# Low parts in quarter tiles, stacked products of the last 16 keys, softmax sums spread by transfers, and an end without GpSimd, in a two-layer attention and retention trunk

## The chip, the cores and the metric

The kernel runs on one core of a Trainium2 chip. The metric is the device time of one execution in microseconds; a figure for a kernel is the median of its runs. Five engines work side by side and meet through semaphores: PE (TensorE, matrix products and transposes), DVE (VectorE), ACT (ScalarE), POOL (GpSimd) and SP (SyncE, which here only issues transfers).

## The reference, cut to what matters

Sixteen learned meta tokens are put ahead of 512 tokens, so every layer has 528 positions of width 1024. Two layers run one after the other:

```python
proj = rmsnorm(h) @ w_in                     # 1024 -> 3*512 + 8 + 4*512 columns
fq, fk, fv, flog, rq, rk, rv, rg = split(proj)
# forgetting attention: 8 heads of 64, c = cumsum(log_sigmoid(flog + b))
s = fq.fk / 8 + c[t] - c[s], causal;  fox = softmax(s) @ fv
# retention: 4 heads of 128, gamma_h ** (t - s), chunked; rq, rk rotated
ret = silu(rg) * groupnorm((rq.rk * decay) @ rv)
h = h + concat(fox, ret) @ w_out
h = h + (silu(rmsnorm(h) @ w_gate) * (rmsnorm(h) @ w_up)) @ w_down
# behind both layers: out = rmsnorm(h)[:, 16:]
```

All of it is float32. The kernel reaches that accuracy with products of split operands: a number is written as a high part, rounded to the short form that TensorE takes at full rate, and a low part, the rest. A product is then high by high, high by low, and low by high, added up in PSUM.

## The kernel before, in words

Tokens lie along the free dimension: `h[k]` holds 128 features by 528 tokens. A dense projection (`dense_steps`, L190) is one job for each 128 output columns: its weights come by a transfer on SP as `raw` (128 partitions by 8 blocks of 128 columns, three buffers), `convert` (L160) casts half of it, 128x512, at a time to the high part `whi` on ACT (L186), and subtracts that from `raw` to get the low part `wlo` (L187). 63 of the 84 dense jobs have `pool` set and do that subtraction on GpSimd, the others on DVE. Then each of eight blocks runs three products, `xh`·`whi`, `xl`·`whi` and `xh`·`wlo`, in two column halves of 264 (L210).

Forgetting attention goes by pairs of heads, g = 0 to 3 (`fox_steps`, L460). For both heads s of a pair, and for query blocks of 128 (in layer 0 with a block of the 16 meta queries ahead), `scores` makes the logits on PE, takes the row minimum of their negative on DVE, and the exponential with its row sum on ACT (L517). `turn` transposes the probabilities on PE and splits them into `pth` and `ptl` (DVE L138). `product` multiplies them with the values `vv`, whose high and low columns lie side by side in one 128-column weight, so that a key block j takes two matmuls (L567; the 16 meta queries have their own, L559). Keys come in four blocks of 128 and one of the last 16 (`KOFF`, `KLEN`). Behind the second head the result is multiplied by the reciprocals of the row sums: they are taken on DVE (L525), spread to 64 columns a head by an ACT copy (L527), turned by four PE transposes (L576), and multiplied from PSUM (L577).

Retention has four heads `hd` (`ret_steps`, L648): scores times the decay (L699), a split into `rsh` and `rsl` (L138), and three products for each key block (L724), for the last 16 keys too, out of tiles of their own (`end_tiles`). Its queries and keys are rotated before that (L608 to L613: two ACT copies, two DVE products and a DVE addition, L613).

The order of PE's instructions is written out by hand: the attention steps of one pair are spread between the dense chunks of the next (`merge`, `spread`), so that PE has dense work while ACT and DVE work on the scores. The order on the other engines comes from a list scheduler with priorities and some pinned instructions. The FFN of each layer (L863 to L1017) uses no GpSimd.

At the end of the last layer (`after_a` to `after_7`, L1135 to L1213) the final norm is laid between the last products of the FFN, in two parts of the tokens: a (272 columns) and b (240). The sums of squares are gathered on DVE (`sum_b`), summed over partitions on PE (`sums`, L1135), and the inverse root is an `Ln` and an `Exp` on ACT (`root`) with a Newton step on DVE (`newton`, L1127 to L1131). The multiplications `out_a` and `out_b` (L1110) go to GpSimd for features 0 to 3 of part a and 6 to 7 of part b, to DVE for the others; SP sends each pair out (L1113).

Of the kernel before, what the change touches and what calls it, by code (L numbers as in the profile page):

```python
# [10 lines left out]
F32 = mybir.dt.float32  # L11
# [28 lines left out]
def hybrid_kernel(ctx, tc, x_t, w_in, w_fl, w_out, w_gate, w_up, w_down, vecs, b_fg, rope, decay, mask, ident, out_t):  # L40
# [25 lines left out]

    p_tiles, t_tiles, pm_tiles, v_tiles, end_tiles, low_keys = [], [], [], [], [], []
# [13 lines left out]
    def enter_att(l):  # L81
# [11 lines left out]
        for t in t_tiles:  # L93
            nc.gpsimd.memset(corners(t).bitcast(F32), 0.0)
        pm_tiles[:] = [phase["att"].tile([32, 32], F32, name=f"pm{i}") for i in range(2)] if l == 0 else []
        for t in pm_tiles:
            zero(l, t)
        end_tiles[:] = [[phase["att"].tile([128, META], F32R, name=f"rs{i}{k}") for k in range(2)] for i in range(2)]
        for t in end_tiles[0] + end_tiles[1]:
            zero(l, t.bitcast(F32))  # L100
# [4 lines left out]
    def corners(t):  # L105
        return t.rearrange("p j c -> p (j c)").rearrange("p (n c) -> p n c", c=META)[:, ::(T + 128) // META]

# [52 lines left out]
    def convert(j, upto=NK, pinned=False):  # L160
# [18 lines left out]
        while job["split"] < min(n, upto):  # L179
# [7 lines left out]
            pin(sub(lo, job["raw"][:, c0:c1], hi.bitcast(F32)), pinned)  # L187
# [209 lines left out]
    def silu(t, last=False):  # L397
        nc.scalar.activation(t, t, AF.Silu)
        if last:
            tc.keep_in_program_order(nc.scalar.preload_act_table_set("natural_log_exp_and_others"))  # L400
# [12 lines left out]
    def fox_dense(l, g, ly, real, st):  # L413
# [32 lines left out]
        def v_done(ps):  # L446
            vt = v_tiles[0]
            for t, (c0, c1) in zip(ps, FULL):
                nc.vector.scalar_tensor_tensor(vt[:, c0:c1], t[:, 0:c1 - c0], RSC, ly["R"][:, c0:c1],
                                               ALU.mult, ALU.mult)  # L450
            st["vt"] = vt
# [8 lines left out]
    def fox_steps(g, st, ly, real):  # L460
# [21 lines left out]
        def scores(s, b):  # L482
# [29 lines left out]
            else:  # L512
                if (s, b) == (0, 0):
                    st["sums"] = tmp.tile([128, NBLK, 2], F32, name="sums", tag="sums")
                rsum = st["sums"][:, b, s:s + 1]
# [8 lines left out]
            elif (s, b) == todo[-1]:  # L524
                nc.vector.reciprocal(st["sums"], st["sums"])  # L525
# [10 lines left out]
        def turn(s, b):  # L536
# [4 lines left out]
            if b < 0:  # L541
                e = at("pe", F32, (32, NBLK, 32), 2)[:, 0]
                nc.vector.transpose(e, info[s, b])
                split(pth[0:META, 0, 0:META], ptl[0:META, 0, 0:META], e[0:META, 0:META])
# [3 lines left out]
            if b == blocks[-1]:  # L548
                split(*[corners(t)[0:META, 1:] for t in (pth, ptl)], st["ends"][0:META, :, 32 - META:32])

        def product(s):
# [4 lines left out]
            if not real:  # L556
                po = psum_a()
                for i, pp in enumerate(pt):
                    nc.tensor.matmul(po[:, 0:META], v[:, 0, :], pp[:, 0, 0:META], start=(i == 0), stop=(i == 1))  # L559
# [4 lines left out]
            for j in range(5):  # L564
                c0 = max(0, KOFF[j] - META)
                for i, pp in enumerate(pt):
                    nc.tensor.matmul(po[:, c0:SEQ], v[:, j, :], pp[:, j, META + c0:T],  # L567
                                     start=(j == 0 and i == 0), stop=(j == 4 and i == 1))
# [3 lines left out]
            if s == 1:  # L572

                rb = psum_a()
                for b in range(NBLK):
                    nc.tensor.transpose(rb[:, 128 * b:128 * b + 128], st["rows"][:, 128 * b:128 * b + 128], idt)  # L576
                nc.vector.tensor_mul(mt[:, META:T], rb, mt[:, META:T])  # L577
# [24 lines left out]
    def ret_dense(l, hd, ly, real, st, which):  # L602
# [17 lines left out]
        def v_done(ps):  # L620
            vr = v_tiles[1]
            nc.vector.scalar_tensor_tensor(sv(vr, False), pv(ps, False), RSC, sv(ly["R"], False), ALU.mult, ALU.mult)
            st["vr"] = vr

        def g_done(ps):
# [3 lines left out]
            if hd > 1:  # L629
                silu(sv(sg, real), True)  # L630
# [17 lines left out]
    def ret_steps(l, hd, st, real):  # L648
# [5 lines left out]
        def values():  # L654
# [3 lines left out]
            for j0, n, p3 in transpose_into(st["vr"], KOFF):  # L658
# [5 lines left out]
                split(vh[:, j0:j0 + n], vl[:, j0:j0 + n], c)  # L664
# [6 lines left out]
        def scores(grp):  # L671
# [32 lines left out]
            if full < used:  # L704
                eh, el = end_tiles[hd % 2]
                split(eh[0:kn], el[0:kn], sd[0:kn, full:used])
                kept["e"] = (eh, el)
            kept["t", grp[0]] = (sh, sl)

        def product(grp):  # L710
# [5 lines left out]
            for j in grp:  # L716
# [4 lines left out]
                if j == 4:  # L721
                    (sh, sl), used = kept["e"], 0
                for i, (a, b) in enumerate(((vh, sh), (vh, sl), (vl, sh))):
                    nc.tensor.matmul(po[:, qa - META:SEQ], a[:, j, :], b[:, used + qa - q0:used + T - q0],  # L724
                                     start=(j == 0 and i == 0), stop=(j == 4 and i == 2))
# [62 lines left out]
    def ffn(l, st, real, last):  # L788
# [93 lines left out]
        class Unit:  # L882
# [64 lines left out]
            def done(self):  # L947
# [6 lines left out]
                silu(sg[:, c], self.f == NF - 1)  # L954
# [103 lines left out]
        else:  # L1058
# [49 lines left out]
            def out(eng, y, r, k, c0, c1):  # L1108
                pair = r.unsqueeze(1).broadcast_to([128, 2, c1 - c0])
                f = eng.tensor_mul(y, y, pair)  # L1110
                if eng is nc.vector:
                    pin(f)
                nc.sync.dma_start(out_t[k:k + 2, :, c0 - META:c1 - META].rearrange("k p c -> p k c"), y)  # L1113

            def out_a(eng, k):
                out(eng, fin["ya"][k // HB][:, k % HB:k % HB + 2], fin["ra"], k, *PA)

            def out_b(eng, k):
                out(eng, fin["yb"][:, k:k + 2], fin["rb"], k, *PB)

            def root(r, v):
                pin(nc.scalar.activation(r, v, AF.Ln, bias=epsc, scale=1.0 / D))
                pin(nc.scalar.activation(r, r, AF.Exp, scale=-0.5))
# [43 lines left out]
            def after_3():  # L1167
                a = fin["ra"], fin["va"], fin["ta"]
                sum_b(2)
                newton(0, *a)  # L1170
                newton(1, *a)
                square_b(3)
                scale_b(0, 1)

            def after_4():
                newton(2, fin["ra"], fin["va"], fin["ta"])
# [226 lines left out]
```

## Time and profile before

| | |
|---|---|
| median of 3 runs | 1278.69 us (1278.58 to 1278.84) |
| the profiled execution | 1278.89 us, its span 1277.1 us |
| mean granted TensorE clock | 0.996 |
| PE busy | 1258.0 us, 99% of the span, 9265 instructions |
| DVE, ACT, POOL busy | 1019.4, 687.7, 181.0 us |
| moved by DMA | 120.55 MB |

The span goes from the first to the last recorded instruction or transfer; the execution's own time is 1.79 us longer than its span. Start times in the views are microseconds from the start of the span. A matmul's recorded duration overlaps that of the next, so what one costs in a stream is read from the distance between the starts. Layer 0's attention lies at about 21 to 282 us, its output projection and FFN at 282 to 650, layer 1's attention at 650 to 905, its projection and FFN behind that, and the end of the last layer from 1248 on.

### The profile page before, as it was taken

Reading aid. Unit: us, or ns where it says so; the run is one execution under the profiler, and the core shown is the slowest. Engines: PE = TensorE matmul, PEld = TensorE weight load, DVE = VectorE, ACT = ScalarE, POOL = GpSimd, SP = SyncE. Lnnn points to the kernel's source line nnn. Section 1 sums busy time; section 2 is a strip of 40 time slices with the busy share of each in tenths; the row PEclk is TensorE's granted clock in tenths of the full one; section 3 lists DMA queues with packets and bytes.
Section 4 is the critical chain, followed back from the end, with each engine's and each line's share of the span. In section 5 each row is a group of like instructions: output and inputs, shape, how many; then the busy total and the mean of one; then the engine's idle time right before and its main releaser. Section 6 shows DMA issues by size and latency. Waiting matters only on the chain.

```text
span 1277.1 us, 23190 instructions
## 1 busy us (share of the span) xinstructions
PE 1258.0 (99%) x9265; PEld 1197.8 (94%) x9265; DVE 1019.4 (80%) x1849; ACT 687.7 (54%) x1250; POOL 181.0 (14%) x150
## 2 busy tenths in 40 slices
PE   9999999999999999999999999999999999999997
PEld 8899999999999999999999989999789999999996
DVE  7888866879988888887687878568899878888867
ACT  7566655576544444444455665456764444444445
POOL 2233333210000000000014334332000000000001
PEclk9999999999999999999999999999999999999998
DMA  6222222223323333332323122222223333333321
GB/s 233 76 67 84 75 84 84 66 73 115 107 97 100 100 100 100 100 100 83 100 76 112 65 100 84 77 91 66 100 83 130 102 100 100 100 100 100 103 79 67
DMA packets 45677, 120.55 MB, mean 94 GB/s; under 512 B 5360, under 2 KB 12272, under 8 KB 45568
## 3 DMA queue, kind: packets, MB, share of 16 engines
q1 hardware_dynamic: 45136, 118.77, 28.4%
q8 instruction: 73, 1.20, 0.4%
q10 hardware_dynamic: 432, 0.29, 0.1%
q14 instruction: 36, 0.29, 0.1%
HBM read 116.91 MB, written 2.13 MB: 93 GB/s over the span
## 4 chain that ended last, share of the span: by engine, by line
PE 84%; DVE 10%; ACT 4%; DMA 1%; issue 1%; DVEq 0%; POOL 0%; ACTq 0%
PE psd L210 24%; PE psa L875 18%; PE psd L1010 14%; PE psd L875 13%; PE psa L1010 4%; PE psa L210 3%; PE psa L409 2%; PE psa L497 1%; PE psa L567 1%; PE psa L724 1%; PE psa L694 1%; DVE qs L429 1%; DMA bc<-cdr 1%; DVE pr L504 1%; DVE rsl L138 0%
## 5 line engine op out<-in xcount | busy, mean ns | idle before, releaser
L187 POOL TENSOR_TENSOR wlo<-raw,whi 128x512 fp32r<-128x512 f32 x126 | 172.3, 1381 | 380.2 <-ACT whi L186 380.2
L210 PE MATMUL psd<-xh,whi 128*128 128x264 f32 (+1 forms) x792 | 195.8, 315 | 0.0
L210 PE MATMUL psd<-xl,whi 128*128 128x264 f32 (+1 forms) x792 | 186.5, 303 | 0.6 <-DVE xl L313 0.6
L210 PE MATMUL psd<-xh,wlo 128*128 128x264 f32 (+1 forms) x792 | 186.9, 303 | 0.0
L210 PEld LDWEIGHTS psd<-xh,whi 128*128 128x128 f32 x792 | 128.7, 190 | 4.7 <-ACT whi L186 0.4
L210 PEld LDWEIGHTS psd<-xh,wlo 128*128 128x128 f32 x792 | 127.2, 188 | 6.2 <-DVE wlo L187 0.4
L210 PEld LDWEIGHTS psd<-xl,whi 128*128 128x128 f32 x792 | 128.0, 189 | 5.2 <-DVE xl L313 1.2
L186 ACT CAST whi<-raw 128x512 fp32r<-128x512 f32 (+1 forms) x168 | 98.3, 613 | 39.2 <-PE psd L210 19.9
L863 ACT CAST whi<-raw 128x1024 fp32r<-128x1024 f32 (+2 forms) x62 | 54.9, 885 | 51.3 <-PE psd L875 39.9
L863 ACT CAST fwhi<-raw 128x1024 fp32r<-128x1024 f32 (+2 forms) x62 | 55.6, 897 | 48.1 <-PE psd L875 40.5
L864 DVE TENSOR_TENSOR wlo<-raw,whi 128x1024 fp32r<-128x1024 f32 (+2 forms) x62 | 62.9, 1014 | 13.7 <-ACT whi L863 13.6
L864 DVE TENSOR_TENSOR fwlo<-raw,fwhi 128x1024 fp32r<-128x1024 f32 (+2 forms) x62 | 64.0, 1032 | 10.8 <-ACT fwhi L863 10.5
L875 PE MATMUL psa<-th,whi 128*128 128x264 f32 (+1 forms) x232 | 65.4, 282 | 0.0
L875 PE MATMUL psa<-th,wlo 128*128 128x264 f32 (+1 forms) x232 | 65.4, 282 | 0.0
L875 PE MATMUL psa<-tl,whi 128*128 128x264 f32 (+1 forms) x232 | 65.3, 282 | 0.0
L875 PE MATMUL psa<-th,fwhi 128*128 128x264 f32 (+1 forms) x224 | 63.4, 283 | 0.0
L875 PE MATMUL psa<-tl,fwhi 128*128 128x264 f32 (+1 forms) x224 | 63.3, 283 | 0.0
L875 PE MATMUL psa<-th,fwlo 128*128 128x264 f32 (+1 forms) x224 | 63.3, 282 | 0.0
L517 ACT ACTIVATE pr<-pr,nmax 128x144 f32<-128x144 f32 (+1 forms) x64 | 36.9, 576 | 42.8 <-DVE nmax L504 30.5
L941 ACT COPY e<-psa 128x264 f32<-128x264 f32 (+1 forms) x114 | 42.9, 376 | 27.9 <-PE psa L875 23.6
L863 ACT CAST fwhi<-S 128x1024 fp32r<-128x1024 f32 x20 | 21.0, 1049 | 68.6 <-PE psa L875 66.5
L1010 PE MATMUL psd<-ah,fwlo 128*128 128x264 f32 (+1 forms) x200 | 56.6, 330 | 0.0
(355 smaller groups left out, 4008.6 us busy)
## 6 DMA issues: line engine op xcount, KB each, us to landing
raw<-w_in SPq DMA_DIRECT2D x54, 512.0 KB, 3.5
raw<-w_gate SPq DMA_DIRECT2D x44, 512.0 KB, 4.0
fraw<-w_up SPq DMA_DIRECT2D x38, 512.0 KB, 3.4
raw<-w_down SPq DMA_DIRECT2D x64, 256.0 KB, 2.7
raw<-w_out SPq DMA_DIRECT2D x16, 512.0 KB, 3.5
raw<-w_down SPq DMA_DIRECT2D x32, 192.0 KB, 2.5
bc<-cdr SPq DMA_DIRECT2D x16, 264.0 KB, 3.3
raw<-w_up SPq DMA_DIRECT2D x6, 512.0 KB, 3.5
```

The source lines that it names most:

```text
L186: pin(nc.scalar.copy(hi, job["raw"][:, c0:c1]), pinned)
L187: pin(sub(lo, job["raw"][:, c0:c1], hi.bitcast(F32)), pinned)
L210: nc.tensor.matmul(ps[1][b][:, 0:c1 - c0], w[:, wk, :], x[:, c0:c1], start=(k == 0 and i == 0), stop=(k == n - 1 and i == 2))
L409: nc.tensor.transpose(ps[:, 128 * j:128 * j + 128], src[:, o:o + 128], idt)
L429: nc.vector.tensor_sub(sv(t, real, b0, b1), sv(tq, real, a0, a1), sv(t, real, a0, a1).bitcast(F32))
L497: nc.tensor.matmul(sc[0:nq, 0:c1 - c0], st["q"][s][:, q0:q0 + nq], kk[:, c0:c1], start=(i == 0), stop=(i == 1))
L517: nc.scalar.activation(pr, pr, AF.Exp, bias=nmax[0:nq], scale=-1.0, accum_out=rsum)
L863: nc.scalar.copy(hi, src)
L864: nc.vector.tensor_sub(lo, src, hi.bitcast(F32))
L875: nc.tensor.matmul(bank()[:, 0:b.shape[-1]], a[:, o + k, :], b, start=(fresh and k == 0 and i == 0), stop=(k == n - 1 and i == 2), skip_gr ...
L941: nc.scalar.copy(self.t["e"][:, i], self.t["x"][:, 0:w])
L1010: nc.tensor.matmul(v[:, 0:c1 - c0], a[:, s * n + k, :], b[:, c0:c1], start=(k == 0 and i == 0), stop=(k == n - 1 and i == 2))
```

## The change

Four parts.

**Low parts in pieces.** Where `convert` subtracts on GpSimd, a half tile of 128x512 is now four instructions of 128x128, one for each block of 128 columns. Those on DVE stay whole.

**Stacked last keys.** A matmul contracts over 128 partitions, and the last 16 keys fill 16 of them. `repeat` now copies the last 16 value columns (before they are transposed) to further places 32 columns apart, so that the transposed values stand on partitions 0, 32, 64, 96 again; the probabilities' high and low parts are put on those partitions of one tile. So the last keys take one matmul in place of two (FoX) or three (retention), and the 16 meta queries one in place of two.

**Softmax sums by transfers.** The reciprocals are turned by a DVE transpose into `turned`, written to DRAM by four small transfers on SP (`rdr`), and read back by two that repeat a row over 64 partitions. The ACT copy and the four PE transposes go; the DVE multiplication reads an SBUF tile in place of PSUM.

**The end.** All of `out_a` and `out_b` are on DVE, at other places; `root` is one `Abs_reciprocal_sqrt`; the subtraction for `sql` comes a step earlier, and the order of the five matmuls of the sum changes.

```diff
 convert
-            pin(sub(lo, job["raw"][:, c0:c1], hi.bitcast(F32)), pinned)
+            step = 1 if job["pool"] else c1 - c0
+            for c in range(0, c1 - c0, step):
+                pin(sub(lo[:, c:c + step], job["raw"][:, c0 + c:c0 + c + step], hi[:, c:c + step].bitcast(F32)), pinned)
 repeat (new), called behind the value projections of FoX and retention
+        nc.scalar.copy(vt[:, at:at + 32 * n].rearrange("p (n c) -> p n c", c=32)[:, :, 0:META],
+                       vt[:, c0:c0 + META].unsqueeze(1).broadcast_to([128, n, META]))
 fox_steps, scores
-                nc.vector.reciprocal(st["sums"], st["sums"])
-                st["rows"] = tt("tq")
-                nc.scalar.copy(st["rows"][:, 0:SEQ].rearrange("p (b s d) -> p b s d", b=NBLK, s=2),
-                               st["sums"].unsqueeze(3).broadcast_to([128, NBLK, 2, 64]))
+                with tc.high_priority():
+                    nc.vector.reciprocal(sums[:, 0:2 * NBLK], sums[:, 0:2 * NBLK])
+                    nc.vector.transpose(turned, sums)
+                rdr = tc.dram_tile([2 * NBLK, 128], F32, name=f"rdr{ly['l']}{g}")
+                for a in range(4):
+                    nc.sync.dma_start(rdr[:, 32 * a:32 * a + 32], turned[32 * a:32 * a + 2 * NBLK, :])
+                st["rows"] = tt("tq")[:, 0:SEQ]
+                wide = rdr.rearrange("(s b) q -> s (b q)", s=2)
+                for i, (a0, a1) in enumerate(ROWS):
+                    nc.sync.dma_start(st["rows"][a0:a1], wide[i:i + 1, :].partition_broadcast(64))
 fox_steps, product
-                for i, pp in enumerate(pt):
-                    nc.tensor.matmul(po[:, 0:META], v[:, 0, :], pp[:, 0, 0:META], start=(i == 0), stop=(i == 1))
+                nc.tensor.matmul(po[:, 0:META], v[:, 4, :], pt[0][:, 4, 0:META], start=True, stop=True)
...
-                for i, pp in enumerate(pt):
+                for i, pp in enumerate(pt if j < 4 else pt[:1]):
...
-                rb = psum_a()
-                for b in range(NBLK):
-                    nc.tensor.transpose(rb[:, 128 * b:128 * b + 128], st["rows"][:, 128 * b:128 * b + 128], idt)
-                nc.vector.tensor_mul(mt[:, META:T], rb, mt[:, META:T])
+                nc.vector.tensor_mul(mt[:, META:T], st["rows"], mt[:, META:T])
 ret_steps, scores and product
-                split(eh[0:kn], el[0:kn], sd[0:kn, full:used])
+                nc.scalar.copy(e[0:kn], d4)
+                nc.vector.tensor_sub(e[32:32 + kn], d4, e[0:kn].bitcast(F32))
+                nc.scalar.copy(e[64:64 + kn], d4)
...
+                    nc.tensor.matmul(po[:, SEQ - META:SEQ], vh[:, 4, :], kept["e"], start=False, stop=True)
 the end of the last layer
-                pin(nc.scalar.activation(r, v, AF.Ln, bias=epsc, scale=1.0 / D))
-                pin(nc.scalar.activation(r, r, AF.Exp, scale=-0.5))
+                pin(nc.scalar.activation(r, v, AF.Abs_reciprocal_sqrt, bias=epsc, scale=1.0 / D))
...
-                out_a(nc.gpsimd, 0)
-                out_a(nc.gpsimd, 2)
...
-                out_b(nc.gpsimd, 6)
-                for k in (0, 2, 4):
-                    out_b(nc.vector, k)
+                for k in range(0, NK, 2):
+                    out_b(k)
```

Three places show how instructions move. Lines behind the change have other numbers: L567 is now L593, L577 is L599, L153 is L162, L1110 is L1142.

On PE, the product of the second head of layer 0's first pair, before:

```order
341 L567 MATMUL psa<-pth,vv_599 128x272
342 L567 MATMUL psa<-ptl,vv_599 128x272
343 L567 MATMUL psa<-pth,vv_599 128x144
344 L567 MATMUL psa<-ptl,vv_599 128x144
345 L567 MATMUL psa<-pth,vv_599 128x16
346 L567 MATMUL psa<-ptl,vv_599 128x16
347 L576 MATMUL psa<-idt,tq 128x128 [waits DVE_49]
348 L576 MATMUL psa<-idt,tq 128x128 x3
349 L724 MATMUL psa<-rsh,rvh 128x400
```

and now:

```order
367 L593 MATMUL psa<-pth,vv_617 128x272
368 L593 MATMUL psa<-ptl,vv_617 128x272
369 L593 MATMUL psa<-pth,vv_617 128x144
370 L593 MATMUL psa<-ptl,vv_617 128x144
371 L593 MATMUL psa<-pth,vv_617 128x16
372 L756 MATMUL psa<-rsh,rvh 128x400
```

The second matmul over the last 16 keys and the four transposes are gone; the four key blocks ahead are as they were, and what followed the transposes follows the product directly.

On SP, the transfers around the sums of the same pair (`rdr` is the DRAM tile, `tq` the spread rows, `bc` the cumulated gates of a head, `raw` a weight tile), before:

```order
32 L153 DMA raw<-w_in 128x1024 [waits DMAHW4_49,Pool_49]
33 L487 DMA bc<-cdr_431 128x528 [waits DMAHW7_49,DVE_49]
34 L153 DMA raw<-w_in 128x1024 [waits DMAHW0_49,Pool_49]
35 L674 DMA dec<-decay 128x528 [waits DVE_49]
36 L153 DMA raw<-w_in 128x1024 [waits DMAHW2_49,Pool_49]
37 L153 DMA raw<-w_in 128x1024 [waits DMAHW3_49,Pool_49]
```

and now:

```order
32 L162 DMA raw<-w_in 128x1024 [waits DMAHW4_49,Activation_49,Pool_49]
33 L504 DMA bc<-cdr_438 128x528 [waits DMAHW7_49,DVE_49]
34 L547 DMA rdr_962<-turned 8x32 [waits DVE_49]
35 L547 DMA rdr_962<-turned 8x32 x2
36 L547 DMA rdr_962<-turned 8x32 [waits DMAHW0_49]
37 L162 DMA raw<-w_in 128x1024 [waits DMAHW1_49,Activation_49,Pool_49]
38 L551 DMA tq<-rdr_962 64x512 [waits DMAHW6_49,DMAHW5_49,DMAHW7_49,DMAHW2_49,DMAHW0_49]
39 L551 DMA tq<-rdr_962 64x512 [waits DMAHW3_49]
40 L702 DMA dec<-decay 128x528 [waits DMAHW4_49,DVE_49]
41 L162 DMA raw<-w_in 128x1024 [waits Activation_49,Pool_49] x2
```

Four writes and two reads stand between the loads; a weight load goes out between the writes and the reads, and the reads wait for the writes to land, with the decay load and two weight loads queued behind them. Weight loads also wait for ACT now beside GpSimd.

On DVE, the end of the program (`th` and `tl` are the output tiles of parts a and b, `S` and `e` hold sums and roots), before:

```order
1801 L1106 TENSOR_TENSOR S<-S,sq 128x240 [waits DVE_49,Activation_49]
1802 L1068 TENSOR_TENSOR h_79<-psa,h_79 128x240 [waits PE_49]
1803 L1068 TENSOR_TENSOR h_80<-psa,h_80 128x240 [waits PE_49]
1804 L1196 TENSOR_TENSOR sql<-S,sqh 128x240 [waits Activation_49]
1805 L1110 TENSOR_TENSOR th_14913<-th_14913,e 128x544 x2
1806 L1127 TENSOR_TENSOR S<-S 128x240 [waits Activation_49]
1807 L1129 SCALAR_TENSOR_TENSOR S<-psa,S 128x240 [waits DVE_49]
1808 L1131 SCALAR_TENSOR_TENSOR S<-S 128x240 [waits DVE_49]
1809 L1110 TENSOR_TENSOR tl_14914<-tl_14914,S 128x480 [waits DVE_49]
1810 L1110 TENSOR_TENSOR tl_14914<-tl_14914,S 128x480
1811 L1110 TENSOR_TENSOR tl_14914<-tl_14914,S 128x480 [waits Activation_49]
```

and now:

```order
1823 L1142 TENSOR_TENSOR th_15315<-th_15315,e 128x544
1824 L1100 TENSOR_TENSOR h_78<-psa,h_78 128x240 [waits PE_49]
1825 L1138 TENSOR_TENSOR S<-S,sq 128x240 [waits DVE_49,Activation_49]
1826 L1100 TENSOR_TENSOR h_79<-psa,h_79 128x240 [waits PE_49]
1827 L1220 TENSOR_TENSOR sql<-S,sqh 128x240 [waits Activation_49]
1828 L1100 TENSOR_TENSOR h_80<-psa,h_80 128x240 [waits PE_49]
1829 L1142 TENSOR_TENSOR th_15316<-th_15316,e 128x544 x2
1830 L1156 TENSOR_TENSOR S<-S 128x240 [waits Activation_49]
1831 L1158 SCALAR_TENSOR_TENSOR S<-psa,S 128x240 [waits DVE_49]
1832 L1160 SCALAR_TENSOR_TENSOR S<-S 128x240 [waits DVE_49]
1833 L1142 TENSOR_TENSOR tl_15317<-tl_15317,S 128x480 [waits DVE_49]
1834 L1142 TENSOR_TENSOR tl_15317<-tl_15317,S 128x480
```

The first two multiplications of part a, GpSimd's before, stand among the additions to `h` now (the second of them is the first row), and four of part b in place of three stand at the very end, the last two of them in a row behind those shown.

More of the change, by code (lines that the diff above doesn't have):

```diff
@@ L65, in hybrid_kernel @@
     nc.vector.memset(onec, 1.0)
+    sum_tiles = [state.tile([128, 32], F32, name=f"sums{i}") for i in range(2)]
+    for t in sum_tiles:
+        nc.gpsimd.memset(t, 0.0)
     p_tiles, t_tiles, pm_tiles, v_tiles, end_tiles, low_keys = [], [], [], [], [], []
@@ L512, in scores @@
             else:
[L513 to L515 removed]
+                rsum = sum_tiles[g % 2][:, NBLK * s + b:NBLK * s + b + 1]
             pr = pt[0:nq, 0:nk]
@@ L548, in turn @@
             if b == blocks[-1]:
-                split(*[corners(t)[0:META, 1:] for t in (pth, ptl)], st["ends"][0:META, :, 32 - META:32])
+                e = st["ends"][0:META, :, 32 - META:32]
+                nc.scalar.copy(corners(pth)[0:META, 1:], e)
+                nc.vector.tensor_sub(corners(ptl)[0:META, 1:4], e[:, 0:3], corners(pth)[0:META, 1:4].bitcast(F32))
+                nc.vector.tensor_sub(pth[32:32 + META, 4, SEQ:T], e[:, 3], pth[0:META, 4, SEQ:T].bitcast(F32))
         def product(s):
```

97 lines of the change are left out of this document (57 added, 40 removed).

## The prediction

> **What bounds the kernel now.** I read the page's totals first, then the chain of work that ended last, then busy times by stage.
>
> ```profile
> span 1277.1 us, 23190 instructions
> PE 1258.0 (99%) x9265; PEld 1197.8 (94%) x9265; DVE 1019.4 (80%) x1849; ACT 687.7 (54%) x1250; POOL 181.0 (14%) x150
> PE 84%; DVE 10%; ACT 4%; DMA 1%; issue 1%; DVEq 0%; POOL 0%; ACTq 0%
> ```
>
> PE is busy for all but 19.1 us of the span, so at most those and PE's own work can go. The windows by stage (span; busy time of PE, weight loads, DVE, ACT, POOL, each with its count; granted clock, DMA share, GB/s) say where:
>
> ```profile
> 21.00:160.00 139.00, 132.48 (x1053) 129.68 (x1052) 113.58 (x269) 84.31 (x200) 45.60 (x34) 0.99 0.26 81
> 160.00:282.00 122.00, 121.84 (x991) 120.66 (x990) 86.17 (x206) 71.21 (x158) 37.71 (x29) 1.00 0.22 72
> 326.00:650.00 324.00, 324.00 (x2669) 324.00 (x2669) 262.77 (x389) 149.09 (x212) 2.87 (x13) 1.00 0.31 99
> 650.00:790.00 140.00, 139.11 (x943) 127.88 (x943) 109.60 (x233) 85.20 (x185) 49.35 (x35) 1.00 0.25 82
> 790.00:905.00 115.00, 114.92 (x715) 102.16 (x714) 78.08 (x175) 66.91 (x138) 39.63 (x30) 1.00 0.24 77
> 1248.00:1277.10 29.10, 19.84 (x156) 18.52 (x154) 20.44 (x42) 15.68 (x39) 4.44 (x3) 0.87 0.21 73
> ```
>
> The change touches the four attention stretches and the end. In the four, PE lacks 6.52, 0.16, 0.89 and 0.08 us, 7.65 together; the FFN, untouched, lacks nothing. So PE sets the time in the attention stretches, and instructions taken off PE there are time won, while waits taken away can bring 7.65 us at most, and a little clock.
>
> **Products and transposes that go.** In the timeline of PE (start, duration, line, operation) the end of one FoX product in layer 0 reads:
>
> ```profile
> 189.02 0.17 PE L559 MATMUL psa<-pth,vv 128*128 128x16 f32 x1
> ...
> 189.16 0.47 PE L567 MATMUL psa<-pth,vv 128*128 128x512 f32 x1
> ...
> 190.50 0.22 PE L567 MATMUL psa<-pth,vv 128*128 128x16 f32 x1
> 190.57 0.26 PE L567 MATMUL psa<-ptl,vv 128*128 128x16 f32 x1
> 190.68 0.65 PE L576 MATMUL psa<-idt,tq 128*128 128x128 f32 x4
> 191.09 0.49 PE L210 MATMUL psd<-xh,whi 128*128 128x264 f32 x2
> ...
> 266.11 0.33 PE L724 MATMUL psa<-rs,rvh 128*128 128x16 f32 x2
> 266.30 0.26 PE L724 MATMUL psa<-rs,rvl 128*128 128x16 f32 x1
> 266.41 0.49 PE L210 MATMUL psd<-xh,whi 128*128 128x264 f32 x2
> ```
>
> Durations overlap, starts tell the price. The four transposes take 191.09−190.68 = 0.41 us, for 4 pairs in 2 layers 8×0.41 = 3.3. The two matmuls of the last 16 keys take 190.68−190.50 = 0.18; half goes, 0.09, for 16 heads 1.4. The pair for the meta queries takes 0.14; half of it, 8 times in layer 0, is 0.6. The retention trio takes 266.41−266.11 = 0.30; two thirds go, 0.20, for 8 heads 1.6. Together 6.9 us, 72 matmuls at some 96 ns. Against this stands a rule: the Trainium skill, "TensorE: Matmul & The Clock Gate", section "Back-to-back issue gap", puts a sustained stream of weight load and 128-column matmul at about 81 ns each, which would be 72×0.081 = 5.8 us as an estimate. I keep the rows, which hold this kernel's own mix. If the freed time is not filled because the next dense chunk then waits for its weights or a free bank, it is lost: a rival below.
>
> **Low parts in pieces.** Groups by line and form (times, mean in ns, idle time ahead and what ended it):
>
> ```profile
> L187 POOL TENSOR_TENSOR wlo<-raw,whi 128x512 fp32r<-128x512 f32 x126 | 172.3, 1381 | 380.2 <-ACT whi L186 380.2
> L358 POOL MEMSET mxh<- 128x512 f32 x2 | 1.0, 524 | 0.0
> L109 POOL MEMSET rs<- 128x16 f32 x4 | 0.2, 104 | 0.0
> L610 DVE TENSOR_TENSOR xsw<-xsw,sr 128x528 f32<-128x528 f32 x12 | 8.5, 707 | 8.1 <-ACT xsw L609 7.9
> L613 DVE TENSOR_TENSOR tq<-tq,xsw 128x528 f32<-128x528 f32 x12 | 12.7, 1060 | 0.1
> ```
>
> No row has a 128-column subtraction. The memsets give (524−104)/496 = 0.85 ns a column and so a fixed part of about 0.09 us; a quarter tile is then (1.381−0.09)/4+0.09 = 0.41 us, with the fixed part doubled 0.50, and a tile 1.65 to 2.0 in place of 1.38: 34 to 78 us more on POOL over 126 tiles. That engine has the room: it sat 380.2 us waiting for ACT's casts in front of these tiles, and in the busiest stretch it works 49.35 of 140 us. It would set the pace only where a job of eight pieces takes longer than PE's 48 matmuls of it, some 5.8 us at the 324.00/2669 = 0.121 us of the FFN window, whose products have the same 264 columns: that is a piece of 0.73 us. PE's third product now waits for a piece in place of a half tile; the first is there 1.38−0.41 = 1 us earlier, the last 0.3 to 0.6 later. I take nothing for that.
>
> A second effect lies on DVE. L610 and L613 are both additions or products of two SBUF tiles of the same shape, yet L613 takes 1060 against 707 ns. One of them, and the tile on POOL beside it:
>
> ```profile
> 56.60 1.28 POOL L187 TENSOR_TENSOR wlo<-raw,whi 128x512 fp32r<-128x512 f32 x1 [1.85 <-ACT whi L186]
> 57.36 1.08 DVE L613 TENSOR_TENSOR tq<-tq,xsw 128x528 f32<-128x528 f32 x1
> 58.36 0.68 DVE L138 TENSOR_TENSOR ptl<-psa,pth 128x512 fp32r<-128x512 f32 x1
> ...
> 59.10 0.51 PE L567 MATMUL psa<-ptl,vv 128*128 128x512 f32 x1 [1.75 <-DVE ptl L138]
> 61.20:64.40 3.20, 3.20 (x16) 3.20 (x16) 1.89 (x7) 0.27 (x1) 0.00 (x0) 0.51 0.02 5
> ```
>
> L613 begins inside the POOL tile and ends 0.56 us behind it, so it stood until that tile was over, and took 0.37 us longer than L610; `ptl`, next on DVE, came late, PE stood 1.75 us, and then ran 3.2 us at a clock of 0.51, another 1.6 lost. The Trainium skill, "SBUF — State Buffer", section "Who interferes with whom", has the port pair that DVE and GpSimd share locked for a whole instruction; the trace agrees in this place. With pieces a DVE operation waits 0.41 us at most, 0.2 in the mean, where it now waits up to 1.28; but POOL is at work some 30% longer, so more operations meet a piece. I expect a third less delay. Of PE's 7.65 us and the 1.6 of clock a share of that size that hangs on DVE is about 2: −2. From below it is all 9.2; from above, with pieces dense enough that every operation meets several, DVE's delay doubles, +4.
>
> **Stacking and its copies.** A copy of 16 columns on ACT, a case shown in
>
> ```profile
> 76.06 0.17 ACT L561 COPY ol<-psa 64x16 f32<-64x16 f32 x1
> ```
>
> stands between the values and their fifth transpose, once a pair and once a retention head, 16 times. If PE waited for each it would be 16×0.17 = 2.7; the transposes of the first four blocks stand ahead of it and cover most. I take +0.5, from 0 to 2.7. The other small copies lie beside dense work, and ACT loses the 128x512 copy of L527.
>
> **The sums.** The chain is reciprocal, DVE transpose, four issues, landing, two reads, landing, multiplication. The tightest of the eight pairs, SP's next issue behind it, and the nearest transfers (a DRAM write in the chain of waits, an issue group with its median landing):
>
> ```profile
> 182.06 0.20 DVE L525 RECIPROCAL sums<-sums 128x8 f32<-128x8 f32 x1
> 184.90 6.27 SPq L153 DMA_DIRECT2D raw<-w_in  x2
> 193.15 0.69 DVE L577 TENSOR_TENSOR mixt<-psa,mixt 128x512 f32<-128x512 f32 x1
> ...
> 34.57 1.48 DMA cdr<-z
> bc<-cdr SPq DMA_DIRECT2D x16, 264.0 KB, 3.3
> ```
>
> From 182.26: transpose 0.3, issues 4×0.33, landing 1.5, so 185.4; the weight load ahead of the reads goes out at 184.90 anyway; two issues and 3.3 for the read give about 189.4. The multiplication starts at 193.15, 3.8 us later, so nothing for the time. A landing twice as slow, 3.0 and 6.6, would bring +1 here. Queued behind the reads on SP are a decay load and weight loads; waiting 1 to 2 us, they are covered by three `raw` buffers. The multiplication now has two SBUF inputs and can meet a piece, 0.4 us with `mxh` behind it; the output that it feeds has a whole pair's time.
>
> **The end.** The chain through the last multiplications:
>
> ```profile
> 1264.12 2.84 POOL L1110 TENSOR_TENSOR th<-th,e 128x544 f32<-128x544 f32 x2 [360.62 <-ACT sq L1103]
> 1264.51 1.25 DVE L1106 TENSOR_TENSOR S<-S,sq 128x240 f32<-128x240 f32 x1
> 1268.60 0.40 ACT L1123 ACTIVATE S<-S 128x240 f32<-128x240 f32 x1
> 1270.36 2.79 DVE L1110 TENSOR_TENSOR tl<-tl,S 128x480 f32<-128x480 f32 x3
> 1270.47 1.60 POOL L1110 TENSOR_TENSOR tl<-tl,S 128x480 f32<-128x480 f32 x1 [3.50 <-DVE S L1131]
> 1272.10 1.97 SPq L1113 DMA_DIRECT2D out_t<-tl  x4
> ```
>
> GpSimd's two multiplications held DVE's sum for 1.25 in place of 0.40 us, −0.85; `Exp` goes, −0.4. DVE takes over two 128x544 multiplications ahead of the sums, half of L1110's pairs at 0.65, of which I let one stand in the way: +0.65. At the end three took 2.79 beside POOL; four at 0.64 take 2.6: −0.2. Sum −0.8; with both multiplications in the way −0.1, with neither −1.5.
>
> **Sum.** −6.9 −2 +0.5 −0.8 = −9.2 against the span of 1277.1, that is 1267.9. The profiled execution took 1278.89, 1.79 more than its span and 0.2 more than the median; so 1269.7, or 1269.5 as a median. The ends: −6.9−9.2−1.5 = −17.6 and −5+4+2.7−0.1+1 = +2.6, with 5 us for the PE term where savings turn into waits; all at once is unlikely.
>
> **Rivals.**
> (1) PE's savings become waits. DVE works 113.58 of 139 us and PE already waits there 6.52. If the savings of the first stretch (a quarter to a third of 6.9) are eaten and the pieces bring nothing, what stays is −4 and −0.8 with +0.5 to +1: about 1274.5. For it: the 1.75 us stand above. Against: the other three stretches have 1.1 us of idle PE.
> (2) The waits fall away. If most of the 9.2 goes, with −6.9 and −0.8, it comes out at about 1263. Against: much of PE's idle time has other causes (transfers, casts).
> (3) Slower: DVE loses more to POOL. A two-input DVE operation that meets a chain of pieces loses up to 0.41 at each, and more operations meet one; in 21 to 160 DVE has only 25 us to spare. It decides when PE's stands in the attention, with the clock that they cost, more than double, from 9.2 by over 8.4; at 2.2 times, +11 −7.7 gives +3, about 1281.5. [...] Against: POOL is not at work without a break (1.85 us idle ahead of the tile at 56.60), and DVE can go in between two pieces.
> (4) The change does less than it says: the small products are covered and only transposes and end count, −4 with +3 of new waits: no difference.
>
> **Chances.** The forecast (1265 to 1273) 0.50; (1) 0.20; (2) 0.12; (3) 0.12; (4) 0.06. The likeliest gives 1269.5. For 8 in 10 I go from 1263, which takes in (2) in part, to 1280, short of (3). A measurement of this kernel tells 0.2%, 2.6 us, from no change: faster is the forecast, (2) and most of (1), together 0.76; same is (4) and the upper end of (1), 0.09; slower is (3) and what I have not seen, 0.15.
>
> **What would show it.** Right: PE 72 matmuls and some 7 us shorter over the four stretches; the transposes' 0.41 gone ahead of L724 or the dense chunk; a piece on POOL at 0.4 to 0.5 us and no wait of PE for `wlo`; L613 nearer 707 than 1060 ns; the multiplication by the sums not waiting for a transfer; the four last multiplications beginning some 8 to 9 us ahead of 1270.36. Wrong: pieces of 0.7 us or more, PE waiting for POOL, a mean of L613 above 1060, a clock below 0.99 in an attention stretch of 160 to 905, or the multiplication released by a transfer.

## The result and the profile after

The changed kernel takes 1272.76 us (1271.47 to 1275.7, 6 runs) against 1278.63 of the kernel before (1277.16 to 1279.1, 6 runs): a ratio of 0.9959 with a 95% interval of [0.9946, 0.9972], so 5.2 us faster, 3.6 to 6.9. The forecast was 1269.5, with 1263 to 1280 as its range. The profiled execution took 1271.97 us, its span 1270.2. Each change in us below is 1278 times the ratio less one, with the ratio taken against runs of the kernel before on the same chip; the column us is the median as measured. The expectations go by differences of medians, so they speak of +2.4 and +5.9 where a table has +1.9 and +6.3. Between two kernels of different tables some 2 us of doubt are left.

The changed kernel's busy times on its page, and its windows by stage (columns as in the prediction):

```profile
PE 1249.5 (98%) x9193; PEld 1189.5 (94%) x9193; DVE 1005.4 (79%) x1874; ACT 691.2 (54%) x1276; POOL 263.7 (21%) x526
```

```profile
21.00:160.00 139.00, 134.33 (x1079) 131.45 (x1078) 111.28 (x287) 88.89 (x217) 73.13 (x136) 1.00 0.28 89
160.00:282.00 122.00, 119.88 (x971) 118.32 (x971) 85.83 (x212) 74.77 (x166) 55.43 (x112) 1.00 0.24 80
650.00:790.00 140.00, 137.74 (x928) 126.44 (x928) 105.12 (x244) 85.68 (x193) 75.32 (x144) 1.00 0.26 89
790.00:905.00 115.00, 113.67 (x698) 100.72 (x697) 77.83 (x174) 69.21 (x144) 55.48 (x112) 1.00 0.24 80
```

PE has 72 instructions less and is busy 8.5 us less, but it stands 4.67, 2.12, 2.26 and 1.33 us in the four attention stretches, 10.38 together, where it stood 7.65. The first stretch has become better (6.52 before), the other three worse. So part of what PE saved turned into waits. The timeline of PE around a FoX product and at the end of a retention product, and then groups of POOL and DVE, all of the changed kernel:

```profile
183.58 0.17 PE L585 MATMUL psa<-pth,vv 128*128 128x16 f32 x1
...
185.02 0.49 PE L221 MATMUL psd<-xh,whi 128*128 128x264 f32 x2
...
261.07 0.22 PE L753 MATMUL psa<-re,rvh 128*128 128x16 f32 x1
261.14 0.49 PE L221 MATMUL psd<-xh,whi 128*128 128x264 f32 x2
```

```profile
L198 POOL TENSOR_TENSOR wlo<-raw,whi 128x128 fp32r<-128x128 f32 x504 | 259.4, 551 | 288.3 <-ACT whi L195 288.3
L635 DVE TENSOR_TENSOR tq<-tq,xsw 128x528 f32<-128x528 f32 x12 | 9.2, 767 | 0.1
```

The FoX product takes 185.02−183.58 = 1.44 us, 0.63 less than the 2.07 before, as worked out (0.41+0.14/2+0.09 = 0.57, and 0.06 over). The retention's last keys take 0.07 in place of 0.30. A piece on POOL takes 551 ns in the mean, more than the 0.41 to 0.50 forecast, but its median of 463 lies inside: some pieces stand (last section). On DVE, the rotation's addition fell from 1060 to 767 ns.

### The profile page after: what moved, and what is told of

It reads as the page before. It is cut to its first block, busy times and chain, and to the rows that moved or that the text cites. A ratio compares the mean times of both kernels' runs of the same rounds, so it can differ in the third digit from the quotient of the medians.

```text
span 1270.2 us, 23608 instructions
## 1 busy us (share of the span) xinstructions
PE 1249.5 (98%) x9193; PEld 1189.5 (94%) x9193; DVE 1005.4 (79%) x1874; ACT 691.2 (54%) x1276; POOL 263.7 (21%) x526
## 4 chain that ended last, share of the span: by engine, by line
PE 85%; DVE 8%; ACT 4%; issue 1%; DMA 1%; DVEq 0%; SPq 0%; ACTq 0%
PE psd L221 25%; PE psa L907 18%; PE psd L1042 14%; PE psd L907 13%; PE psa L1042 4%; PE psa L221 4%; PE psa L423 1%; PE psa L593 1%; PE psa L514 1%; PE psa L756 1%; PE psa L722 1%; PE psa L384 1%; ACT whi L195 1%; DVE ptl L147 1%; DVE pr L521 1%
## 5 line engine op out<-in xcount | busy, mean ns | idle before, releaser
L198 POOL TENSOR_TENSOR wlo<-raw,whi 128x128 fp32r<-128x128 f32 x504 | 259.4, 551 | 288.3 <-ACT whi L195 288.3
```

The costliest lines, as they stand in the source:

```text
L198: pin(sub(lo[:, c:c + step], job["raw"][:, c0 + c:c0 + c + step], hi[:, c:c + step].bitcast(F32)), pinned)
```

## The experiments

**Each part alone.** The kernel before with one of the four parts of the change, and nothing else.

> Only GpSimd's low parts in pieces of 128 columns; the rest as before. Theory A (pieces pay: DVE's additions of two SBUF tiles stand shorter behind GpSimd, and PE's stands get shorter; a tile of four pieces takes 4 x 0.45 = 1.8 us or more and holds up a weight load on SP at the start of layer 1, 1 us): between -2.5 and -0.5 us, the rotation's last addition (L613 before) falls from 1060 to about 770 ns. Theory B (pieces cost: the tile ends later, and weight loads on SP that wait for GpSimd, with the gates' transfers behind them, come later, more than the DVE side brings): +0.5 to +3 us, with the same fall of the addition.

> Only the stacked products of the last 16 keys and of the meta queries; the rest as before. Theory A (PE sets the time, a small matmul costs the distance between starts): 40 matmuls fewer take 3.6 us off PE, the copies give back 0.5, so -3.1 us. Theory B (savings on PE in layer 0's first stretch turn into waits, and the repeats hold up the fifth transpose of the values): -1.5 us or less, with new PE stands ahead of the transposes of the values.

> Only the softmax sums by transfers; the rest as before. Theory A: 32 transposes fewer take 8 x 0.41 = 3.3 us off PE and the transfers stay hidden: -3.3 us, the multiplication by the sums never released by a transfer. Theory B (six more transfers a pair on SP hold up weight loads or the gates' transfers queued behind them): -1.5 us or less, with PE or ACT standing for a weight tile or DVE for the gates' rows behind the sums' transfers.

> Only the new end of the last layer; the rest as before. Theory A (as forecast): -0.8 us. Theory B (the changed kernel's end is only about 0.2 us shorter, counted from the last matmul of the output projection, because the last matmuls of the sum now wait longer for DVE): -0.3 to 0 us.

| part alone | us | ratio | 95% interval | change |
|---|---|---|---|---|
| pieces | 1272.43 | 0.9960 | [0.9948, 0.9972] | −5.1 us |
| stacked keys | 1280.08 | 1.0015 | [1.0007, 1.0024] | +1.9 us |
| sums by transfers | 1283.53 | 1.0049 | [1.0035, 1.0064] | +6.3 us |
| the end | 1277.66 | 0.9997 | [0.9988, 1.0005] | −0.4 us |

I had expected the opposite shares: the two parts that take work off PE are slower alone, and the one that gives GpSimd more work carries the gain. Theory A fell for the stack and the sums, and B for the pieces, whose gain is larger than A had it. The end's interval holds both theories. One place where PE loses in the sums alone is the last pair; the timelines of DVE, POOL and PE of that kernel:

```profile
888.00 1.27 DVE L141 TENSOR_TENSOR rvl<-sq,rvh 128x128 fp32r<-128x128 f32 x1 [0.26 <-ACT rvh L140]
889.19 1.14 DVE L141 TENSOR_TENSOR ptl<-psa,pth 128x384 fp32r<-128x384 f32 x2
887.85 2.54 POOL L190 TENSOR_TENSOR wlo<-raw,whi 128x512 fp32r<-128x512 f32 x2 [2.63 <-ACT whi L189]
890.39 0.50 PE L576 MATMUL psa<-ptl,vv 128*128 128x512 f32 x1 [2.03 <-DVE ptl L141]
```

A subtraction of 128x128 from two SBUF tiles takes 1.27 us because it begins 0.15 after a whole tile on POOL began (the two tiles of the row take 1.27 each); `ptl` comes behind it, and PE stands 2.03. In the kernel before the same small subtraction went ahead of that tile and PE had no stand there. The scheduler's order of DVE is another in this kernel, and with whole tiles a bad place costs about a microsecond. It is this order, and not a weight load as theory B had it, that PE stands for here.

**Parts undone, and a piece of another size.** The changed kernel with one part put back, and the kernel before with two pieces of 256 columns:

```diff
+            step = 2 if job["pool"] else c1 - c0
```

> The changed kernel with GpSimd's low parts in whole tiles of 128x512 again. The parts alone gave +2.4 (stacked products), +5.9 (sums) and 0.0 us (end). Theory A (the parts add up, whatever the pieces do): +8.3 us against the kernel before, about 1286. Theory B (both lose by the same thing, DVE operations of two SBUF tiles that are put elsewhere by the scheduler and stand up to 1.3 us behind a whole tile, so that together they lose less than the sum): +3 to +6 us, 1281 to 1284. Theory C (they save PE 7 us and only a chance order cost it alone): below +1 us.

> The changed kernel with the softmax sums spread by the ACT copy and four PE transposes again. Theory A (the sums' transfers cost what they cost alone, 5.9 us): -11 us against the kernel before, about 1267. Theory B (behind pieces the transfers are hidden and the transposes' 3.3 us count): 3 us slower than the changed kernel, about 1275.5. Between them: within 1 us of the changed kernel.

> The changed kernel with two or three matmuls for the last 16 keys again. Theory A (the stack costs what it costs alone, 2.4 us): 2 us faster than the changed kernel, about 1270. Theory B (behind pieces it saves PE's 3.6 us): 3 us slower than the changed kernel, about 1275.5.

> The kernel before with GpSimd's low parts in two pieces of 128x256 in place of four. Theory A (the gain of 5.2 us comes from shorter stands of DVE behind GpSimd, up to one piece, with more instructions as the price): between a half and all of it, -2.6 to -5 us, and the rotation's addition between 767 and 1060 ns, near 850. Theory B (the gain comes from PE having the first block earlier): like A with 256, but the addition's mean would not matter; then PE's waits for wlo in the kernel before must be as large as the gain.

| kernel | us | ratio | 95% interval | change |
|---|---|---|---|---|
| changed, whole tiles | 1282.16 | 1.0032 | [1.0020, 1.0043] | +4.1 us |
| changed, sums by PE | 1270.66 | 0.9945 | [0.9932, 0.9957] | −7.0 us |
| changed, no stack | 1273.17 | 0.9964 | [0.9952, 0.9977] | −4.6 us |
| before, pieces of 256 | 1274.13 | 0.9968 | [0.9956, 0.9981] | −4.1 us |

Without pieces the other three parts make the kernel 4.1 us slower, less than the 7.8 they cost one by one: the size is theory B's of that run, its reason was not taken apart. With pieces the sums cost about 2 us (−7.0 against −5.2, the intervals overlap) and the stack nothing or a small gain, between the theories in both; neither brings the 3 us that its PE time is worth. The pieces' gain follows the length of what DVE can meet. The rotation's addition, in the groups of the kernel with pieces of 256 columns, then of 128 alone, and last what the waits of PE's weight loads for `wlo` are in the kernel before (total, times, longest):

```profile
L615 DVE TENSOR_TENSOR tq<-tq,xsw 128x528 f32<-128x528 f32 x12 | 10.8, 904 | 0.1
```

```profile
L615 DVE TENSOR_TENSOR tq<-tq,xsw 128x528 f32<-128x528 f32 x12 | 9.5, 790 | 0.1
```

```profile
PEld psa L210 <- POOL wlo L187: 0.5, 1, 0.5
```

1060, 904 and 790 ns go with 0, −4.1 and −5.1 us; the step from 256 to 128 is within the intervals. That PE has a first block earlier can't be it: it waited 0.5 us for `wlo`, once, in the whole kernel before. Nor can it be a lucky order: cutting the tiles moves nothing else. By the traces PE, DVE, ACT and SP run the same operations on the same tiles in the same order in the kernel before, with two pieces and with four. What changes beside POOL's tiles is DVE's own time, by 20.6 us from 1019.4 for the same 1849 instructions, as the page of the kernel with the pieces alone has it:

```profile
PE 1254.7 (99%) x9265; PEld 1196.4 (94%) x9265; DVE 998.8 (79%) x1849; ACT 688.5 (54%) x1250; POOL 270.4 (21%) x528
```

The changed kernel and that with whole tiles have equal orders too, and 1005.4 against 1028.5 us on DVE.

**Where the sums' gain went.** Against the kernel with PE's transposes, the changed kernel wins about 0.4 us at each pair on PE and loses 1.1 us near 70, 1.8 near 249 and 1.2 near 881. Near 249, the timelines of PE and DVE of the changed kernel, and then DVE's of the kernel with the sums by PE, which lies 1.1 us earlier up to this place (`sd` is the product of retention scores and decay, `mean` a sum over the next values):

```profile
249.49 0.30 PE L423 MATMUL psa<-idt,pd 128*128 128x128 f32 x1 [1.21 <-DVE sd L727]
248.31 0.69 DVE L685 TENSOR_REDUCE mean<-psa 128x4 f32<-128x512 f32 x1 [0.75 <-PE psa L423]
248.92 0.42 DVE L727 TENSOR_TENSOR sd<-psa,dec 128x264 f32<-128x264 f32 x1
```

```profile
243.92 1.20 DVE L722 TENSOR_TENSOR sd<-psa,dec 128x264 f32<-128x264 f32 x3
```

`sd` runs 5.0 us later by the starts, 3.9 with that shift taken off, and DVE stood 0.75 us in front of `mean` with `sd` behind it in its order. PE's transpose needs the PSUM bank that `sd` frees. The order on DVE, without the instructions for the sums, has `sd` one to five places later near 67, 126, 249 and 870, and where it was at most of the other places. The spread sums and `sd` share a ring of four buffers (`tq`, `sd` and others), and the sums' buffer is taken ahead of `sd` in the program; its first writer is now a transfer that waits for two others, where it was an ACT copy right behind the reciprocals. I took this for the cause and put the taking of the buffer and the two reads into a function `read_rows`, called a step later in the program:

```diff
-                st["rows"] = tt("tq")[:, 0:SEQ]
...
+                st["rdr"] = rdr
...
+            if (s, b) == todo[-1]:
+                read_rows()
```

PE's order stays the same and DVE's and ACT's change. SP's changes at the last pair alone, where a weight load goes out ahead of the two reads, at 871.57 in place of 877.68.

> The changed kernel in which the buffer of the spread sums is taken, and the two reads are written, a step later in the program (ahead of the last turn); SP's order stays what it was, DVE's decay products of the retention scores (sd) come three to nine places earlier in layer 0. Theory A (the sums lose their gain because the buffer, one of four shared with sd, is taken ahead of sd, and the scheduler then puts sd late on DVE; PE stands for sd's PSUM bank): the stands of 1.21 us near 249 and of 0.60 together near 70 go, 1.5 to 3 us faster than the changed kernel. Theory B (the six transfers themselves hold up weight loads on SP): no change within 0.7 us, and the stands stay.

**The start of layer 1.** One of the two longest stands of PE in the changed kernel, 1.65 us each, is at 679.84. The timelines of PE, POOL and DVE, the same place of PE in the kernel before, and then the chain of waits that leads to the stand:

```profile
679.84 0.30 PE L423 MATMUL psa<-idt,pd 128*128 128x128 f32 x1 [1.65 <-DVE vv L491]
668.07 0.89 POOL L198 TENSOR_TENSOR wlo<-raw,whi 128x128 fp32r<-128x128 f32 x2
663.64 1.40 DVE L404 TENSOR_TENSOR_SCAN z<-z 8x528 f32<-8x528 f32 x1
675.70 0.31 DVE L521 CUSTOM_DVE_ANT_0 pr<-psa,bc 128x144 f32<-128x144 f32 x1 [3.00 <-DMA bc<-cdr]
```

```profile
684.69 0.30 PE L409 MATMUL psa<-idt,pd 128*128 128x128 f32 x1 [0.64 <-DVE vv L474]
```

```profile
668.98 0.33 SPq L162
669.31 0.05 issue
669.36 3.08 DMA cdr<-z
672.44 0.02 issue
672.46 3.11 DMA bc<-cdr
675.57 0.03 issue
675.60 0.02 DVEq L521
675.62 0.09 issue
675.70 0.31 DVE pr L521
```

The gates (`z`) are ready when DVE's scan ends at 665.04, but their write to DRAM goes out at 669.36: on SP a weight load stands ahead of it, which needs a buffer that POOL empties with its eighth piece, the second of the row of two, which end at 668.96. The first scores wait for the rows read back (`bc`), and PE for the scores. In the kernel before the same load stood there, but went out when POOL's second tile of that job ended: the write followed the scan's end by 2.2 us, not 4.3, and PE stood 0.64. With the pieces alone PE stands 1.80 at this place, about the loss of 1 us that theory A of that run had there. So here the longer way of a tile in pieces does reach PE, through SP. ACT can issue the write instead:

```diff
-        nc.sync.dma_start(st["cdr"], z2)
+        (nc.scalar if l else nc.sync).dma_start(st["cdr"], z2)
```

> The changed kernel with the ACT copy and the four PE transposes for the sums, and the write of layer 1's cumulated gates to DRAM issued by ACT in place of SP. Theory A (at the start of layer 1 that write stands on SP behind a weight load that waits for GpSimd's last piece, and PE then stands for the first scores): the write goes out 3 to 4 us earlier, the rows of the gates land as much earlier, PE's stand near 680 goes: 1 to 2 us faster than without this (that was 1270.7), so about 1269.2. Theory B (the stand has another cause, the weight tile or the PSUM bank): no change within 0.7 us.

> The changed kernel with both: the spread sums' buffer taken later, and layer 1's gates written by ACT. If both theories A hold, the gains add: 2.5 to 5 us faster than the changed kernel, 1267.5 to 1270.

| kernel | us | ratio | 95% interval | change |
|---|---|---|---|---|
| changed, rows later | 1268.00 | 0.9921 | [0.9908, 0.9935] | −10.1 us |
| changed, sums by PE, gates by ACT | 1268.92 | 0.9930 | [0.9918, 0.9943] | −8.9 us |
| changed, rows later, gates by ACT | 1265.01 | 0.9903 | [0.9887, 0.9918] | −12.4 us |

Theory A held for the sums, and brought 4.9 us in place of 1.5 to 3: the stands near 70, 249 and 881 are gone, the last of which I had not counted (there SP's order changed as well, so the cause is not separated at that pair). The transfers themselves cost nothing that shows: of the two kernels with the gates by ACT, the one with the transfers is 3.5 us ahead, about the 3.3 us of the transposes. For the gates the expected sign came in both kernels, −1.9 and −2.3 us, inside the intervals by time. The trace decides: ACT's issue, SP's reads and DVE's first use of the rows in the last kernel,

```profile
661.58 0.53 ACTq L406 DMA_DIRECT2D cdr<-z  x1
665.93 0.90 SPq L504 DMA_DIRECT2D bc<-cdr  x2
670.10 0.31 DVE L521 CUSTOM_DVE_ANT_0 pr<-psa,bc 128x144 f32<-128x144 f32 x1 [0.85 <-DMA bc<-cdr]
674.14 0.71 PE L423 MATMUL psa<-idt,pd 128*128 128x128 f32 x5
```

where the write goes out 4.35 us ahead of the reads, DVE waits 0.85 for the rows in place of 3.00, and PE has no stand at all there. This kernel is faster than both: 12.4 us ahead of the one before, 7.2 of the changed one, more than the 2.5 to 5 expected. Neither edit was tried on the kernel before, where the write also stood 2.2 us on SP, so the 12.4 us are not the change's alone.

**Whole tiles in the good order.** The last kernel with `step = c1 - c0`:

> The kernel with the rows' buffer taken later and the gates written by ACT (1265.0 us), with GpSimd's low parts in whole tiles of 128x512 again. Theory A (the pieces are worth the same in any order, by shorter stands of DVE behind GpSimd, 4 to 5 us as in the kernel before): about 1269.5, and the rotation's addition back near 1000 ns. Theory B (on top of the other parts they are worth 9 us, as between the changed kernel and that without pieces, since DVE has more operations of two SBUF tiles on PE's path there): about 1274.

It takes 1275.46 us, 0.9969 [0.9958, 0.9980]: 8.4 us slower than with pieces. The size is theory B's: the pieces are worth 5 us in the kernel before and 8 to 9 in the changed one. Theory B's reason, more operations of two SBUF tiles on PE's path, is not shown: DVE's time differs by 22.7 us here, hardly more than the 20.6 of the kernel before. The windows show where PE loses, those of this kernel and then the first stretch with pieces:

```profile
21.00:160.00 139.00, 129.66 (x1021) 126.05 (x1020) 115.11 (x270) 85.93 (x208) 44.22 (x32) 0.99 0.27 85
160.00:282.00 122.00, 121.44 (x982) 119.91 (x981) 90.31 (x218) 72.64 (x167) 39.69 (x30) 1.00 0.26 77
```

```profile
21.00:160.00 139.00, 134.98 (x1089) 132.58 (x1088) 112.64 (x292) 89.44 (x220) 75.03 (x139) 1.00 0.29 91
```

PE stands 9.34 us in the first stretch, 4.02 with pieces, and hardly in the next. The rotation's addition is back at 986 ns. All engines but POOL run in the same order in both.

## Why the prediction was right, and where it was not

The time fell as forecast and inside the range, but partly by luck: the term that was to bring most of the gain brought none by itself, and a term of −2 brought more than twice its size.

**Products and transposes, −6.9.** The price was right: the FoX and the retention product shown became shorter by about what was worked out (0.63 against 0.57, 0.23 against 0.20). The rows' price held, not the lower 5.8 us that the prediction set against it. PE's total of 8.5 us does not show it, since the pieces alone, which take no instruction off PE, lower it by 3.3 (1258.0 to 1254.7). What failed is the step that instructions taken off PE are time won: alone, the stack and the sums gained nothing, and in the changed order the stack shows 0.6 us of its 3.6, inside the intervals. Only with the rows taken later do the transposes' 3.3 us arrive (3.5 between the two kernels with the gates by ACT).

**The end, −0.8.** Right by the trace. From the last FFN product to the end of the span it took 1277.10−1265.37 = 11.73 us, and now 1270.20−1259.37 = 10.83 (that product before, then three rows of the changed kernel):

```profile
1265.37 0.28 PE L875 MATMUL psa<-ah,fwlo 128*128 128x240 f32 x1
1259.37 0.28 PE L907 MATMUL psa<-ah,fwlo 128*128 128x240 f32 x1
1264.39 2.36 DVE L1142 TENSOR_TENSOR tl<-tl,S 128x480 f32<-128x480 f32 x4
1265.11 2.04 SPq L1143 DMA_DIRECT2D out_t<-tl  x4
```

Four multiplications take 2.36 us without GpSimd beside them, where three took 2.79. The runs can't tell 0.9 us from none. The four begin 6.0 us earlier than the three did; 8 to 9 was named as the sign of a right forecast.

**Stands by DVE's delay behind POOL, −2.** The mechanism was right and its size was not: the pieces alone bring −5.1. The windows of that kernel, the four stretches:

```profile
21.00:160.00 139.00, 136.48 (x1107) 134.51 (x1107) 110.92 (x284) 89.04 (x210) 75.77 (x139) 1.00 0.27 87
160.00:282.00 122.00, 121.51 (x989) 120.47 (x988) 83.42 (x204) 73.94 (x159) 55.35 (x111) 1.00 0.24 75
650.00:790.00 140.00, 138.20 (x939) 127.44 (x939) 103.03 (x236) 84.08 (x185) 74.87 (x144) 1.00 0.27 84
790.00:905.00 115.00, 114.99 (x716) 102.72 (x715) 76.09 (x169) 69.36 (x139) 55.70 (x112) 1.00 0.24 76
```

PE stands 2.52, 0.49, 1.80 and 0.01 us, 2.8 less than before. Four stands in layer 0 shrink, that near 59 from 1.75 to 0.71 and those of 0.88, 1.14 and 0.90 near 95, 108 and 157 to under 0.3; the one at the start of layer 1 grows from 0.64 to 1.80. The slow clock near 61 is absent too, but can't be put down to the pieces: it is also absent in the kernel with the new end alone, whose tiles are uncut and whose stand is as long (last section). I let a third of DVE's delay go; the addition's excess over the 707 ns of L610 fell by three quarters, from 353 to 83.

**The sums, and the later end of a tile, both at nothing.** These two steps failed. The transfers are hidden, with the multiplication waiting for none of them, but the buffer that they fill, taken ahead of `sd`, moved `sd` on DVE: taking it later brings 4.9 us. And the later end of a tile reaches PE at the start of layer 1, not as a wait for `wlo` but through a weight load on SP with the gates' write behind it: PE's stand there grows from 0.64 to 1.65 us. With both mended the kernel is 12.4 us faster than before, more than the forecast; how much of that either edit would bring without the change was not run.

**Rival (1)**, savings that turn into waits, is in part what happened, and the time lies between the forecast and its 1274.5, but not as it was told: the first stretch got better, and the stands came in the other three. **Rival (3)**, slower because DVE loses more behind POOL, did not come: DVE's time fell from 1019.4 to 1005.4 us. The chance of "faster" rested on the parts adding up; they don't, and without the pieces the other three come out 4.1 us slower.

**Left open.** The stack alone costs 1.9 us, with longer stands of PE before transposes of values and for `ptl`, about as its theory B had it, but which of its copies moves them was not taken apart. Why the pieces are worth 8 to 9 us in the changed order and 5 in the one before, with DVE's time falling about as much in both, is not known either.

## What to carry to other kernels

Where PE is busy 99% of the time, taking instructions off it pays only as long as nothing on the other engines moves later: compare the order on the engines that wait before counting the gain, above all where a new tile comes out of a ring shared with others, since a buffer taken early for a slow transfer delays what is taken behind it. A long GpSimd operation that reads SBUF was a price here for the DVE operations of two SBUF tiles that met it; cutting it up cost GpSimd time that it had, and lowered the price. A queue that issues transfers in order turns a wait for one engine into a wait for all: keep a small urgent transfer, like the gates' write that stood 4.3 us here, off a queue on which a load waits for a buffer.

## What the runs showed of the hardware

The delay goes both ways: two pieces on POOL that began at 663.47, while DVE ran a scan and a subtraction of SBUF tiles, took together 2.50 us, where the two above at 668.07 take 0.89 (timelines of the changed kernel):

```profile
663.47 2.50 POOL L198 TENSOR_TENSOR wlo<-raw,whi 128x128 fp32r<-128x128 f32 x2 [6.83 <-ACT whi L195]
664.97 1.56 DVE L457 TENSOR_TENSOR kl<-tq,kh 64x528 fp32r<-64x528 f32 x2
```

The scan is the one above at 663.64. One of these two is the longest of all 504 pieces, 2.07 us; the median is 463 ns, the mean 551. The Trainium skill, "SBUF — State Buffer", section "Who interferes with whom", has the one that issues second block until the first is through; the trace agrees in this place.

A stand of PE does not always cost clock. At the same place near 59, a stand of 1.75 us was followed by 3.2 us at a granted clock of 0.51 in the kernel before, and one of the same length by a clock of 1.00 in the kernel with the new end alone, whose tiles are uncut too:

```profile
58.90 0.50 PE L570 MATMUL psa<-ptl,vv 128*128 128x512 f32 x1 [1.75 <-DVE ptl L138]
61.00:64.20 3.20, 3.20 (x29) 3.20 (x28) 2.92 (x10) 1.39 (x3) 0.42 (x1) 1.00 0.12 32
```

So of two equal stands one costs 1.6 us more, and a single profile can't tell which is the rule. The nine executions of the kernel before that stand beside the last table fall into two groups: six took 1277.2 to 1277.9 us at a mean granted clock of 0.998, three 1279.1 to 1279.2 at 0.996 to 0.997. That this place makes the difference is not shown.
